# A decoder trunk in split fp32: lent weight slots in forgetting attention, and one weight split ahead of the last softmax

## The chip, the core and the metric

The kernel runs on one core of one Trainium2 chip. The metric is the device time of the program in microseconds (us), as a median of several runs. Engines are named as the profile names them: PE (TensorE matmul), PEld (its weight load), DVE (VectorE), ACT (ScalarE), POOL (GpSimd), SP (SyncE, which issues nearly all DMAs).

## The reference

Sequence 256, width 1024, two layers. Layer 0 mixes with forgetting attention (FoX, 16 heads of 64), layer 1 with multi-head latent attention (MLA, 16 heads, 128 + 64 wide). Every layer is

```python
x = post_norm(x, 0.5 * swiglu(x, ffn1_w_in[i], ffn1_w_out[i]), ln_g[i, 0], ln_b[i, 0])
mix = fox_mixer(...) if i < N_A else mla_mixer(...)
x = post_norm(x, mix, ln_g[i, 1], ln_b[i, 1])
x = post_norm(x, 0.5 * swiglu(x, ffn2_w_in[i], ffn2_w_out[i]), ln_g[i, 2], ln_b[i, 2])
gate = sigmoid(x @ ple_w_gate[i] + ple_b_gate[i])
x = post_norm(x, gate * (p[i] @ ple_w_proj[i]), ln_g[i, 3], ln_b[i, 3])
```

where post_norm is layer_norm(ALPHA * x + delta). FoX's logits are q.k / sqrt(64) plus a running sum of log sigmoid gates; both attentions are causal softmaxes. All in float32.

## The kernel before, in words

**Split arithmetic.** Every float32 operand of a matmul is written as a high part (rounded to the format fp32r) and a low part (the rest). A product is three matmuls: high x high, high x low, low x high (`mm3`). So each weight that arrives from HBM has to be split before TensorE can use it: ACT copies it rounded into the high half of a buffer (line 194, or 202 when only this half is issued), DVE subtracts this from the raw weight into the low half (line 195, or 206). One such split of a 128x1024 weight is called a split below. Activations are split in the same way (lines 499 and 500).

**Buffers.** Raw weights land in three buffers `raw`, 1 MB each, two weights to a buffer. Split weights go into slots: ten fixed ones `hl0` to `hl9`, and buffers of other use that are lent for a time (`S.lend`) and taken back (`S.reclaim`): `ota` and `otb` (later the attention's output), `qk` (later the heads' q and k) and `fs` (scratch of the FoX gates). A slot comes free when the last matmul that reads it is issued; the list of free slots is first in, first out.

**The order of the work.** The program is written out once, with a planner (class `Stream`) that decides where splits stand. After nearly every matmul group it asks (`pump`): is a slot free, has the next raw weight arrived by the planner's clock, are ACT and DVE not too far behind? If so, the next split is issued there, on ACT and on DVE. A finished pair of splits frees a raw buffer and issues the next load on SP. So the splits run ahead of TensorE as far as slots allow. In parts where ACT and DVE have other urgent work, `S.hold` turns this off, and splits stand where the code says. In MLA a list of steps (`ORDER`) says everything: `f n` splits whatever keeps the next n weights ready, `a` issues the ACT half of one split, `l` the DVE half, `sm h` is the softmax of head h (two min-reductions on DVE, line 1466, then two exponentials on ACT, line 1471), `div h 0` divides by the sums (DVE, lines 1480 and 1483), `T h` transposes the result P on TensorE and splits it into `PT`, `AV h` multiplies by V, `O h t` by one weight of the output projection, for half t of the 256 tokens.

**FoX.** It follows the first FFN. That FFN ends with the layer norm of the first 128 tokens, the transposes of these tokens into `xT` in two halves (each split on ACT and DVE), and the layer norm of the other 128. FoX then makes V in pieces: `VA(0)`, `VC(0)` (with the transposes of the other 128 tokens inside), `VB(0)`, `VC(1)`, `VB(1)`, `VA(1)`. `VC` also gives the gates' logits, which go through a chain of small steps on ACT, POOL and DVE in `fs` (lines 944 to 979). Then `gen_k` and `gen_q` make k and q of two heads at a time into `qk`, and the softmaxes follow; `AV(j)` writes the output into `ota` (j below 4) and `otb` (j from 4 on), lines 1114 and 1117.

Before, `qk` and `fs` are taken back in the first FFN (at its chunk 8), `ota` and `otb` where FoX begins.

Of the kernel before, what the change touches and what calls it, by code (L numbers as in the profile page):

```python
# [11 lines left out]
F32R = mybir.dt.float32r  # L12
# [61 lines left out]
)  # L74
# [16 lines left out]
class Recorder:  # L91
# [10 lines left out]
    lend = reclaim = check = load = busy = pair = split = split_pieces = ahead = later = split_now = fill = pump  # L102
# [295 lines left out]
class Trunk:  # L398
# [459 lines left out]
    def fox(self, li):  # L858
        nc, S, a = self.nc, self.S, self.a
        v = {}  # L860
        S.reclaim("ota", "otb")

        def VA(t):

            ps = self.bank("h" if t == 0 else "y")
            self.moving(ps, t, ("fv",), 512)
            o = v[t, 0] = self.tl([128, 2, 512], F32R, "g4", 5)
            self.parts(o[:, 0, :], o[:, 1, :], ps)

        def VB(t, what=None):  # L870

            ps = self.bank("h" if t == 0 else "y")
            for k in range(8):
                if k == 1 and what:
                    what()
                if k % 4 == 0:
                    w = self.use(("fvb", k // 4))
                c = 256 * (k % 4)
                self.mm3(
                    ps[:, 0:256], lambda i: self.xT[:, t, i, k, :], lambda i: w[:, i, c : c + 256], k == 0, k == 7)  # L880
            if (t, 1) not in v:
                v[t, 1] = self.tl([128, 2, 512], F32R, "g4", 5)
            o = v[t, 1]
            self.parts(o[:, 0, 0:256], o[:, 1, 0:256], ps[:, 0:256])

        def VC(t, at={}):

            ps = self.bank("y")
            for k in range(8):
                if k in at:  # L890
                    at[k]()
                if k % 3 == 0:
                    w = self.use(("fvc", k // 3))
                c = 272 * (k % 3)
                self.mm3(
                    ps[:, 0:272], lambda i: self.xT[:, t, i, k, :], lambda i: w[:, i, c : c + 272], k == 0, k == 7)
            if (t, 1) not in v:
                v[t, 1] = self.tl([128, 2, 512], F32R, "g4", 5)
            o = v[t, 1]
            nc.scalar.activation(ftok[:, t, 112:128], ps[:, 256:272], AF.Copy)  # L900
            self.parts(o[:, 0, 256:512], o[:, 1, 256:512], ps[:, 0:256])
# [15 lines left out]
        fs = self.own([128, 2048], F32, "fs")  # L917
# [15 lines left out]
        f, e, u, r, ab = (fs[fr, 256 * i : 256 * i + 256] for i in range(5))  # L933
# [60 lines left out]
        VC(0, {4: lambda: self.XT(1, (0,)), 7: lambda: self.XT(1, (1,))})  # L994
        VB(0)
        VC(1)
        VB(1, gates)
        VA(1)

        st, PT = {}, {}  # L1000
        qk = self.own([128, 2, 2, 512], F32R, "qk")
        OT = [self.own([128, 4, 2, 256], F32R, tag) for tag in ("ota", "otb")]

        def gen(j, key, c0, hold):
            ps = self.bank("h")
# [4 lines left out]
        def gen_k(j):  # L1010
            gen(j, "fk", 256, j >= 2)

        def gen_q(j):
            gen(j, "fq", 0, j >= 2)

        def QK(j, ring):
            sb = [self.bank(ring) for _ in range(2)]
            half = [slice(0, 64), slice(64, 128)]
            o = qk[:, j % 2]
            for s in range(2):  # L1020
                h = 2 * j + s
                self.mm(
                    sb[s][:, 0:384], sel[half[s], h : h + 1].to_broadcast([64, 128]), negc[half[s], :],
                    True, False,
                )
            for n, (i, jj) in enumerate(((0, 0), (0, 1), (1, 0))):
                for q0, c0, c1 in ((0, 0, 128), (128, 128, 384)):
                    for s in range(2):
                        self.mm(
                            sb[s][:, c0:c1], o[half[s], i, q0 : q0 + 128],  # L1030
                            o[half[s], jj, 256 : 256 + c1 - c0], False, n == 2 and q0 > 0,
                        )
            st[j] = sb
# [20 lines left out]
        def exps(j):  # L1054
            sb, tt = st[j]
            su = self.tl([128, 4], F32, "su", 2)
            pair = self.tl([128, 768], F32, "P", 2)
            P = [pair[:, 384 * s : 384 * s + 384] for s in range(2)]
            for s in range(2):
                for q, (c0, c1) in enumerate(seg):  # L1060
                    i = 2 * s + q
                    nc.scalar.activation(
                        P[s][:, c0:c1], sb[s][:, c0:c1], AF.Exp, bias=tt[:, i : i + 1], scale=-1.0,
                        accum_out=su[:, i : i + 1],
                    )
            self.S.busy(act=1800)
            st[j] = P, su
# [28 lines left out]
        def AV(j, what=None):  # L1096
            o = PT.pop(j)
            ps = self.bank("h" if j != 5 else "tr")
            n, c = j // 4, 128 * (j % 4)
            strided = ps.rearrange("p (s c) -> p s c", s=2)[:, :, 128:256]  # L1100
            for m, (i, jj) in enumerate(((0, 0), (0, 1), (1, 0))):
                self.mm(ps, v[0, n][:, i, c : c + 128], o[:, jj, 0:512], m == 0, False)
            for m, (i, jj) in enumerate(((0, 0), (0, 1), (1, 0))):
                self.mm(
                    strided, v[1, n][:, i, c : c + 128],
                    o[:, jj, 512:768].rearrange("p (s c) -> p s c", s=2), False, m == 2,
                )
            if what:
                what()
            ot = OT[j // 4][:, j % 4]  # L1110
            self.S.busy(act=700, dve=600)
            for s in range(2):
                r = slice(64 * s, 64 * s + 64)
                nc.scalar.activation(ot[r, 0, :], ps[r, 256 * s : 256 * s + 256], AF.Copy)
            for s in range(2):
                r = slice(64 * s, 64 * s + 64)
                nc.vector.tensor_tensor(
                    ot[r, 1, :], ps[r, 256 * s : 256 * s + 256], ot[r, 0, :].bitcast(F32), op=ALU.subtract
                )
# [5 lines left out]
        def O(k, t):  # L1125
# [3 lines left out]
            for n in range(2):  # L1129
                if t == 1 and k == 7:  # L1130
                    self.XT(0, (n,))
                self.mm3(
                    y[t][n], lambda i: OT[k // 4][:, k % 4, i, 128 * t : 128 * t + 128],
                    lambda i: w[:, i, 512 * n : 512 * n + 512], k == 0, k == 7,
# [8 lines left out]
        for a in range(0, 6, 2):  # L1143
            if a == 2:
                self.load_gb(li, 1)
            QK(a, "y")
            QK(a + 1, "y")
            least(a)
            if a:
                AV(a - 1)  # L1150
            exps(a)
            S.ahead()
            least(a + 1)
            gen_k(a + 2)
            exps(a + 1)
            divide(a)
            S.later()
            gen_q(a + 2)
            divide(a + 1)
            S.split_now()  # L1160
            S.split_now()
            gen_k(a + 3)
            T(a)
            S.split_now()
            gen_q(a + 3)
            AV(a)
            T(a + 1)
# [100 lines left out]
    def mla(self, li):  # L1268
# [231 lines left out]

        OT = []

        def ot_of(h):
            if h >= 14:
                return self.kvt[:, 512 * (h - 14) : 512 * (h - 13)].rearrange("p (i c) -> p i c", i=2)
            return OT[h >= 10][:, (h + 2 * (h >= 10)) % 4]

        def AV(h):
            if h in (0, 10):
                OT.append(self.own([128, 4, 2, 256], F32R, "ota" if h else "otb"))  # L1510
            o = PT.pop(h)
# [45 lines left out]
    def run(self):  # L1557
        S = self.S
        keep = lambda *t: (lambda: S.reclaim(*t))
        ple = lambda li: {  # L1560
            4: [keep("ota")],
            6: [lambda: self.ple_load(li)],
        }
        self.ffn(0, "ffn1", 0, at={3: [self.load_x], 8: [keep("qk", "fs")]}, cold=True)
        self.fox(0)
        self.ffn(0, "ffn2", 2, ple=True, at=ple(0))
        self.load_gb(0, 3)
        self.kv_setup()
        self.ple(0, False)
        S.reclaim("fs")  # L1570
        self.ffn(1, "ffn1", 0, kv=True, at={10: [keep("ota")]})
        self.mla(1)
        self.ffn(1, "ffn2", 2, ple=True, at=ple(1))
        self.load_gb(1, 3)
        self.ple(1, True)
# [94 lines left out]
```

## Time and profile before

| what | value |
|---|---|
| median of three runs | 1072.36 us (1070.35 to 1072.91) |
| the profiled execution | 1070.54 us |
| its span, first to last instruction | 1068.8 us |
| mean granted TensorE clock | 0.997 |
| PE busy | 1057.0 us (99%), 7236 matmuls |
| DVE busy | 717.7 us (67%) |
| ACT busy | 541.8 us (51%) |
| POOL busy | 64.6 us (6%) |
| HBM read | 197.40 MB, 186 GB/s over the span |

How to read it: "busy" is the union of an engine's instructions. Matmuls are pipelined, so one that waits a little still overlaps the one before it; a lost moment on PE shows in the distance from the start of one group to the start of the next. In a timeline row stand the start, the duration, engine, line, operation, what is written from what, its shape and how many equal instructions follow each other; in brackets the engine's idle time before it and what ended that. The FoX stage lies at about 188 to 303 us, MLA at about 711 to 848 us.

### The profile page before, as it was taken

How to read it: one execution, taken by the hardware profiler on the slowest of the kernel's cores; microseconds unless marked ns; L12 is line 12 of the kernel's file. 1: busy time of each engine (PE TensorE's matmuls, PEld its weight loads, DVE VectorE, ACT ScalarE, POOL GpSimd, SP SyncE). 2: the span in 40 equal slices, each digit the busy share in tenths (PEclk: the TensorE clock that was granted, in tenths of full speed). 3: DMA queues.
4: the chain of work that ended last, by engine and by line, in shares of the span. 5: the costliest groups of instructions: out<-in, count | busy, mean ns of one | idle time of the engine just before them, and what ended most of it. 6: DMA issues, size and time to landing. Idle time of an engine off the chain costs nothing.

```text
span 1068.8 us, 17497 instructions
## 1 busy us (share of the span) xinstructions
PE 1057.0 (99%) x7236; PEld 969.8 (91%) x7236; DVE 717.7 (67%) x1029; ACT 541.8 (51%) x805; POOL 64.6 (6%) x94
## 2 busy tenths in 40 slices
PE   9999999999999999999999999999999999999996
PEld 8989998899889999998899999989999789898986
DVE  6675545878797545548966454578887886454566
ACT  5654433667645534444555453436675466354431
POOL 0000000233200000000320000000000000000000
PEclk9999999999999999999999999999999999999998
DMA  8886642543347755354477555423434568555502
GB/s 298 327 286 226 242 161 83 200 163 147 119 163 289 265 192 189 141 201 148 175 277 266 182 188 182 153 71 109 148 135 153 197 239 310 178 209 179 190 5 79
DMA packets 33091, 199.58 MB, mean 187 GB/s; under 512 B 3698, under 2 KB 5490, under 8 KB 12148
## 3 DMA queue, kind: packets, MB, share of 16 engines
q1 hardware_dynamic: 33012, 198.47, 51.5%
q8 instruction: 57, 0.93, 0.3%
q14 instruction: 22, 0.18, 0.0%
HBM read 197.40 MB, written 1.05 MB: 186 GB/s over the span
## 4 chain that ended last, share of the span: by engine, by line
PE 96%; DVE 1%; issue 1%; ACT 1%; POOL 0%; DMA 0%; SPq 0%; DVEq 0%; POOLq 0%; ACTq 0%
PE y L490 36%; PE h L490 35%; PE tr L490 23%; PE tr L494 2%; DMA raw<-in_w_dram 0%; PE h L494 0%; PE tr L1086 0%; ACT hl L194 0%; DVE x L575 0%; POOL fs L957 0%; POOL fs L950 0%; SPq L360 0%; SPq L476 0%; DVE hl L195 0%; ACT P L1471 0%
## 5 line engine op out<-in xcount | busy, mean ns | idle before, releaser
L195 DVE TENSOR_TENSOR hl<-raw,hl 128x1024 fp32r<-128x1024 f32 (+3 forms) x263 | 309.2, 1195 | 143.1 <-ACT hl L194 142.4
L194 ACT ACTIVATE hl<-raw 128x1024 fp32r<-128x1024 f32 (+3 forms) x263 | 266.1, 1033 | 173.8 <-PE y L490 94.8
L490 PE MATMUL h<-xT,hl 128*128 128x256 f32 x1560 | 184.8, 278 | 1.5 <-ACT hl L232 1.2
L490 PEld LDWEIGHTS h<-xT,hl 128*128 128x128 f32 x1560 | 181.0, 188 | 2.8 <-ACT hl L232 1.5
L490 PE MATMUL y<-hl,g 128*128 128x512 f32 x780 | 182.3, 390 | 0.0
L490 PE MATMUL tr<-xT,hl 128*128 128x256 f32 x1512 | 176.6, 277 | 0.0
L490 PEld LDWEIGHTS tr<-xT,hl 128*128 128x128 f32 x1512 | 174.2, 188 | 0.5
L490 PEld LDWEIGHTS y<-hl,g 128*128 128x128 f32 x780 | 145.4, 188 | 29.5
L490 PE MATMUL h<-hl,xT 128*128 128x512 f32 (+2 forms) x300 | 67.6, 377 | 0.0
L490 PE MATMUL y<-hl,xT 128*128 128x512 f32 (+3 forms) x348 | 64.1, 334 | 0.0
L490 PEld LDWEIGHTS h<-hl,xT 128*128 128x128 f32 x300 | 53.6, 188 | 10.2
L490 PEld LDWEIGHTS y<-hl,xT 128*128 128x128 f32 x348 | 53.5, 188 | 6.3 <-ACT xT L499 0.4
L567 POOL TENSOR_TENSOR rs<-ve,mhalf 128x1 f32<-128x1 f32 x16 | 15.1, 942 | 625.9 <-DVE ve L566 625.9
L500 DVE TENSOR_TENSOR g<-P,g 128x512 fp32r<-128x512 f32 x38 | 26.3, 692 | 26.5 <-ACT g L499 26.5
L490 PE MATMUL y<-hl,otb 128*128 128x512 f32 x168 | 42.9, 396 | 0.0
L499 ACT ACTIVATE xT<-tr 128x512 fp32r<-128x512 f32 x28 | 16.2, 597 | 51.0 <-PE tr L494 50.9
L499 ACT ACTIVATE g<-P 128x512 fp32r<-128x512 f32 x38 | 24.0, 632 | 32.8 <-DVE P L684 32.8
L195 DVE TENSOR_TENSOR otb<-raw,otb 128x1024 fp32r<-128x1024 f32 (+1 forms) x21 | 25.3, 1204 | 16.7 <-ACT otb L194 16.7
L195 DVE TENSOR_TENSOR qk<-raw,qk 128x1024 fp32r<-128x1024 f32 (+2 forms) x22 | 26.6, 1211 | 14.5 <-ACT qk L194 14.4
L490 PEld LDWEIGHTS y<-hl,otb 128*128 128x128 f32 x168 | 30.2, 188 | 5.6
L683 ACT ACTIVATE P<-tr 128x512 f32<-128x512 f32 x20 | 12.0, 599 | 44.5 <-PE tr L490 44.5
L684 DVE TENSOR_TENSOR P<-P,tr 128x512 f32<-128x512 f32 x20 | 13.8, 688 | 30.0 <-PE tr L490 15.2
(262 smaller groups left out, 1432.0 us busy)
## 6 DMA issues: line engine op xcount, KB each, us to landing
raw<-in_ffn_in_dram SPq DMA_DIRECT2D x85, 1024.0 KB, 5.0
raw<-in_ffn_out_dram SPq DMA_DIRECT2D x44, 1024.0 KB, 5.0
raw<-in_pg_dram SPq DMA_DIRECT2D x8, 1024.0 KB, 4.8
raw<-in_mo_dram SPq DMA_DIRECT2D x8, 1024.0 KB, 4.8
raw<-in_kq_dram SPq DMA_DIRECT2D x8, 640.0 KB, 4.0
gb<-in_ln_g_dram SPq DMA_DIRECT2D x8, 512.0 KB, 7.0
gb<-in_ln_b_dram SPq DMA_DIRECT2D x8, 512.0 KB, 7.7
raw<-in_fk_dram SPq DMA_DIRECT2D x4, 1024.0 KB, 5.2
```

Of the source, the lines that this page charges most:

```text
L194: nc.scalar.activation(hi, src, AF.Copy)
L195: nc.vector.tensor_tensor(lo, src, hi.bitcast(F32), op=ALU.subtract)
L490: self.nc.tensor.matmul(out, lhsT, rhs, start=start, stop=stop)
L494: self.nc.tensor.transpose(out, in_, self.ident)
L499: self.nc.scalar.activation(hi, src, AF.Copy)
L500: self.nc.vector.tensor_tensor(lo, src, hi.bitcast(F32), op=ALU.subtract)
L567: nc.gpsimd.tensor_tensor(rs, ve, self.mhalf, op=ALU.pow)
L683: nc.scalar.activation(gt, ps[0], AF.Silu)
L684: nc.vector.tensor_tensor(gt, gt, ps[1], op=ALU.mult)
```

## The change

Three edits to where buffers are lent, and one to the list of steps.

1. `qk` stays lent until FoX begins and is taken back there; `ota` is taken back after `VC(1)`, `otb` at the second pair of heads (where the next layer norm's weights are loaded), and the tiles in `ota` and `otb` are made where `AV` first writes them. `fs` is taken back at chunk 10 of the first FFN.
2. In MLA, the split of the last output weight is issued as `a` ahead of `O 13 0` and `sm 15`, and its DVE half as `l` behind `sm 15`; before it stood as a whole (`f 2`) behind `sm 15`.

```diff
-    "f 1", "div 14 0", "l", "O 12 0", "AV 13", "O 6 1", "f 2", "QK 15", "T 14", "lend", "O 13 0", "sm 15",
-    "f 2", "div 15 0", "l", "AV 14", "O 7 1", "f 3", "O 8 1", "gb", "T 15", "f 4", "O 9 1", "AV 15", "O 14 0",
+    "f 1", "div 14 0", "l", "O 12 0", "AV 13", "O 6 1", "f 2", "QK 15", "T 14", "lend", "a", "O 13 0", "sm 15",
+    "l", "div 15 0", "AV 14", "O 7 1", "f 3", "O 8 1", "gb", "T 15", "f 4", "O 9 1", "AV 15", "O 14 0",
...
     def fox(self, li):
-        S.reclaim("ota", "otb")
+        S.reclaim("qk")
...
         VC(1)
+        S.reclaim("ota")
         VB(1, gates)
...
-        OT = [self.own([128, 4, 2, 256], F32R, tag) for tag in ("ota", "otb")]
+        OT = []
...
+            if j % 4 == 0:
+                OT.append(self.own([128, 4, 2, 256], F32R, "otb" if j else "ota"))
             ot = OT[j // 4][:, j % 4]
...
                 self.load_gb(li, 1)
+                S.reclaim("otb")
...
-        self.ffn(0, "ffn1", 0, at={3: [self.load_x], 8: [keep("qk", "fs")]}, cold=True)
+        self.ffn(0, "ffn1", 0, at={3: [self.load_x], 10: [keep("fs")]}, cold=True)
```

No instruction is added or taken out on PE, ACT, DVE, POOL or SP, apart from what follows from names; PE, POOL and SP keep their order, and PE reads some weights from other slots. What moves are splits on ACT and DVE.

**The end of MLA, on ACT.** P, su and nm are the probabilities, the sums and the minima of a softmax, PT the transposed and split probabilities, `fs` here the output of head 14. Before, from the split of the weight ahead of it to the head's output:

```order
L194 ACTIVATE hl9_8382<-raw_8156 128x1024
L499 ACTIVATE PT_8400<-tr_8396 128x384
L1471 ACTIVATE P_8411,su_8410<-tr_8385,nm_8409 128x128
L1471 ACTIVATE P_8411,su_8410<-tr_8385,nm_8409 128x256
L194 ACTIVATE hl6_8416<-raw_8156 128x1024
L499 ACTIVATE fs_6382<-h_8424 128x256
```

and in the changed kernel (line 1475 is line 1471 of before):

```order
L194 ACTIVATE hl6_8382<-raw_8156 128x1024
L499 ACTIVATE PT_8400<-tr_8396 128x384
L202 ACTIVATE hl2_8403<-raw_8156 128x1024
L1475 ACTIVATE P_8413,su_8412<-tr_8385,nm_8411 128x128
L1475 ACTIVATE P_8413,su_8412<-tr_8385,nm_8411 128x256
L499 ACTIVATE fs_6382<-h_8424 128x256
```

The copy of the last output weight has moved from behind the two exponentials to ahead of them. On DVE the order is as it was: the two reductions of the softmax, the subtraction of this weight, the reciprocal, the divisions.

**The start of FoX, on ACT.** `xT` is the transposed input, `g4` a piece of V, raw widths of 544 and 1024 are weights. Before, from the last splits of V's weights to the second pair of `xT` halves:

```order
L194 ACTIVATE hl4_1859<-raw_1611 128x544
L194 ACTIVATE hl5_1867<-raw_1723 128x1024
L194 ACTIVATE hl6_1876<-raw_1723 128x1024
L499 ACTIVATE xT_72<-tr_1881 128x512
L499 ACTIVATE xT_72<-tr_1891 128x512
L194 ACTIVATE hl7_1901<-raw_1788 128x1024
L499 ACTIVATE g4_1956<-h_1931 128x512
L499 ACTIVATE xT_72<-tr_1972 128x512
L194 ACTIVATE hl8_1985<-raw_1788 128x1024
L499 ACTIVATE xT_72<-tr_1993 128x512
```

and in the changed kernel:

```order
L194 ACTIVATE hl3_1790<-raw_1611 128x544
L194 ACTIVATE hl4_1864<-raw_1699 128x1024
L194 ACTIVATE hl5_1873<-raw_1699 128x1024
L499 ACTIVATE xT_72<-tr_1881 128x512
L194 ACTIVATE hl6_1891<-raw_1755 128x1024
L499 ACTIVATE xT_72<-tr_1894 128x512
L499 ACTIVATE g4_1956<-h_1931 128x512
L194 ACTIVATE hl7_1972<-raw_1755 128x1024
L499 ACTIVATE xT_72<-tr_1977 128x512
L194 ACTIVATE hl8_1993<-raw_1793 128x1024
L499 ACTIVATE xT_72<-tr_1996 128x512
```

Here the splits of the first two weights of k (hl6 and hl7, before hl7 and hl8) have each moved ahead of an `xT` half, and the first weight of q (hl8) stands ahead of the last half. The 544-wide split stands ahead of the layer norm's work on DVE in the changed kernel; before it stood behind it:

```order
L575 SCALAR_TENSOR_TENSOR x0_66<-x0_66,mv_1828,gb_648 128x512
L575 SCALAR_TENSOR_TENSOR x0_66<-x0_66,rs_1830,gb_648 128x512
L195 TENSOR_TENSOR hl4_1859<-raw_1611,hl4_1859 128x544
L195 TENSOR_TENSOR hl5_1867<-raw_1723,hl5_1867 128x1024
L195 TENSOR_TENSOR hl6_1876<-raw_1723,hl6_1876 128x1024
L500 TENSOR_TENSOR xT_72<-tr_1881,xT_72 128x512
L500 TENSOR_TENSOR xT_72<-tr_1891,xT_72 128x512
L195 TENSOR_TENSOR hl7_1901<-raw_1788,hl7_1901 128x1024
L556 SCALAR_TENSOR_TENSOR x1_67<-x1_67,y_110 128x512
```

(DVE before, from the end of the first layer norm to the start of the second), and in the changed kernel:

```order
L575 SCALAR_TENSOR_TENSOR x0_66<-x0_66,mv_1833,gb_648 128x512
L575 SCALAR_TENSOR_TENSOR x0_66<-x0_66,rs_1835,gb_648 128x512
L195 TENSOR_TENSOR hl4_1864<-raw_1699,hl4_1864 128x1024
L195 TENSOR_TENSOR hl5_1873<-raw_1699,hl5_1873 128x1024
L500 TENSOR_TENSOR xT_72<-tr_1881,xT_72 128x512
L195 TENSOR_TENSOR hl6_1891<-raw_1755,hl6_1891 128x1024
L500 TENSOR_TENSOR xT_72<-tr_1894,xT_72 128x512
L556 SCALAR_TENSOR_TENSOR x1_67<-x1_67,y_110 128x512
```

One subtraction fewer stands between the two layer norms, and one of 1024 now stands between the two halves of `xT`.

From there to about 373 us every split stands where the split of the weight before it stood: the kernel is one weight further ahead. The order of all other work on these engines is the same.

## The prediction

> **What bounds the kernel now.** I read the page first, then the waits of PE alone, then timelines of the places where splits move. On the page one engine is busy all the time, and the chain of work that ended last runs through it.
>
> ```profile
> span 1068.8 us, 17497 instructions
> PE 1057.0 (99%) x7236; PEld 969.8 (91%) x7236; DVE 717.7 (67%) x1029; ACT 541.8 (51%) x805; POOL 64.6 (6%) x94
> PE 96%; DVE 1%; issue 1%; ACT 1%; POOL 0%; DMA 0%; SPq 0%; DVEq 0%; POOLq 0%; ACTq 0%
> ```
>
> The changed kernel has the same matmuls, so only moments in which PE waits can be won. The view of PE's waits has four groups. Three belong to the program's first 9 us, which the change does not touch (one is shown), and one does not:
>
> ```profile
> PE y L466 <- POOL mhalf L450: 1.2, 1, 1.2
> ...
> PE tr L494 <- DVE P L1483: 0.8, 1, 0.8
> ```
>
> That is a single wait near the end of MLA: the transposes of the last head (T 15) wait for the division of its softmax. Shorter waits show only as a longer distance between the starts of groups, so I looked for these in timelines. In no group after the first 9 us does PE wait for a weight's split. Being one weight further ahead in FoX can therefore win nothing by itself; it can only shift what ACT and DVE do at the few places where PE is close behind them.
>
> **The start of FoX.** The timeline from the end of the first layer norm:
>
> ```profile
> 184.66 2.99 DVE L195 TENSOR_TENSOR hl<-raw,hl 128x544 fp32r<-128x544 f32 x3
> ...
> 186.19 0.60 ACT L499 ACTIVATE xT<-tr 128x512 fp32r<-128x512 f32 x1 [2.10 <-PE tr L494]
> ...
> 187.57 1.28 DVE L500 TENSOR_TENSOR xT<-tr,xT 128x512 fp32r<-128x512 f32 x2
> ...
> 187.82 1.68 PE L490 MATMUL h<-ota,xT 128*128 128x512 f32 x6
> 188.90 1.22 DVE L195 TENSOR_TENSOR hl<-raw,hl 128x1024 fp32r<-128x1024 f32 x1
> 189.33 1.54 PE L490 MATMUL h<-otb,xT 128*128 128x512 f32 x6
> 190.04 0.68 DVE L556 SCALAR_TENSOR_TENSOR x<-x,y 128x512 f32<-128x512 f32 x1
> 190.71 2.91 PE L490 MATMUL h<-hl,xT 128*128 128x512 f32 x12
> ```
>
> The first six matmuls of VA(0) take 189.33 - 187.82 = 1.51, the next six 190.71 - 189.33 = 1.38, or 0.23 each. So 0.13 is lost: the third matmul needs the low half of xT, which DVE starts at 187.57, behind three subtractions. One of them, 544 wide (about 0.6 of the 2.99), is done before the layer norm now, so this low half starts near 186.95. Gain **0.10**.
>
> Against that, a weight of k is now split between the two halves of xT: copied on ACT from 186.79 (186.19 + 0.60) for about 1.05, and subtracted on DVE for 1.22. The second half's high part starts at 187.85 and its low part ends near 187.85 + 1.22 + 0.68 = 189.75; before it ended at 188.85. PE's first reader is the third unit of VA(0), at 190.71, and wants the low part two matmuls later, at 191.17. That leaves 1.4, so the edit costs nothing; were the cover gone, it would cost at most the 1.22. The second pair of halves is used by VC(1), 10 us later, with one subtraction more ahead of it: the same price, more cover. The second layer norm starts 0.3 before 190.04; what follows it may win a tenth, which I do not count (from 0 to 0.2).
>
> From there on each split stands at an old place, one weight ahead. ACT's and DVE's queues hold as much work as before at each of them, and each load is issued sooner, since raw buffers come free sooner. Price zero, covered by PE's distance to its weights. Making the output tiles late, and `otb` holding a weight until then, puts no wait on AV, which writes it two pairs of heads later. For `fs` at chunk 10, the same weight is its last in both kernels.
>
> **The last softmax.** The timeline of MLA's end:
>
> ```profile
> 827.95 0.49 ACT L499 ACTIVATE PT<-tr 128x384 fp32r<-128x384 f32 x1 [0.91 <-PE tr L494]
> ...
> 829.08 0.80 PE L490 MATMUL h<-PT,g 128*128 128x256 f32 x6
> ...
> 829.67 0.14 DVE L1466 DVE_READ_ACCUMULATOR2_ANT nm<- 128x1 f32 x1
> 829.72 2.95 PE L490 MATMUL y<-hl,otb 128*128 128x512 f32 x12
> 829.85 0.37 ACT L1471 ACTIVATE P<-tr,nm 128x128 f32<-128x128 f32 x1 [1.41 <-DVE nm L1466]
> ...
> 830.56 0.20 ACT L1471 ACTIVATION_READ_ACCUMULATOR P<-tr,nm 128x1 f32 x1
> 830.66 1.05 ACT L194 ACTIVATE hl<-raw 128x1024 fp32r<-128x1024 f32 x1
> ...
> 831.74 1.22 DVE L195 TENSOR_TENSOR hl<-raw,hl 128x1024 fp32r<-128x1024 f32 x1 [1.93 <-ACT hl L194]
> ...
> 832.88 0.16 DVE L1480 RECIPROCAL su<-su 128x2 f32<-128x2 f32 x1
> 833.08 0.55 DVE L1483 TENSOR_SCALAR P<-P,su 128x128 f32<-128x128 f32 x2
> ...
> 833.51 0.61 PE L494 MATMUL tr<-ident,P 128*128 128x128 f32 x3 [0.84 <-DVE P L1483]
> 833.54 0.42 DVE L500 TENSOR_TENSOR fs<-h,fs 128x256 fp32r<-128x256 f32 x1
> 833.87 1.22 DVE L195 TENSOR_TENSOR hl<-raw,hl 128x1024 fp32r<-128x1024 f32 x1
> 833.88 1.64 PE L490 MATMUL y<-hl,otb 128*128 128x512 f32 x6
> 834.22 0.49 ACT L499 ACTIVATE PT<-tr 128x384 fp32r<-128x384 f32 x1 [1.28 <-PE tr L494]
> ...
> 835.01 0.55 DVE L500 TENSOR_TENSOR PT<-tr,PT 128x384 fp32r<-128x384 f32 x1
> 835.35 1.05 PE L490 MATMUL h<-PT,g 128*128 128x256 f32 x6
> ```
>
> The sums of the softmax are there at 830.76 (830.56 + 0.20), yet DVE's reciprocal starts at 832.88. Ahead of it in DVE's queue stands the subtraction of a weight, and that waits for its copy, which ACT makes only behind the exponentials. PE's twelve 512-wide matmuls from 829.72 take 12 x 0.23 = 2.76, so T 15 could have started at 832.48; it started at 833.51. PE loses **1.03**.
>
> Now the copy stands ahead of the exponentials. ACT is done with PT at 828.44 and idle for 1.41 until 829.85. The copy takes 1.05 and ends at 829.49, 0.36 before the exponentials can start, so they lose nothing. Its raw weight is the other half of a buffer that was split from a head earlier. DVE's last reduction ends at 829.81; the subtraction runs from there to 831.05, beside the exponentials, and the reciprocal starts at 831.05, 1.83 earlier. The transposes could start at 833.51 - 1.83 = 831.68, and PE gets to them at 832.48. So the whole 1.03 goes, with 0.8 to spare. On SP the load that this split frees, and the next layer norm's two loads behind it, issue up to 1.9 earlier in the same order; POOL has nothing here.
>
> What is late next is head 15's AV. Its six matmuls took 1.05, those of head 14 0.80: 0.25 is lost, since the second matmul needs the low half of PT, which ended at 835.56. In the new order T 15 and PT's copy come 1.03 earlier; the copy ends at 833.68. On DVE the divisions end at 831.8, then follow 0.42 and a subtraction of 1.22, so it is free at about 833.45, and the low half ends near 834.25. AV 15 starts at 832.85 + 1.38 = 834.23 and its second matmul about 0.1 later. I take **0.20** of the 0.25.
>
> **The sum.** 0.10 + 1.03 + 0.20 = 1.33 us, all of it PE's own waiting. The profiled execution took 1070.54 (its span, and 1.7 around it), and becomes 1069.2. The median of the runs stands 1.82 above that execution: 1072.36 - 1.33 = **1071.0**, 0.12% less. The three runs lie 0.24% apart (1070.35 to 1072.91), so 0.3% (3.2 us) is about what a measurement can tell from no change.
>
> **Rivals.** *A race on the gates' chain.* FoX's gates share DVE with the first k and q:
>
> ```profile
> 212.20 11.68 PE L490 MATMUL h<-xT,hl 128*128 128x256 f32 x96
> ...
> 213.78 0.74 POOL L956 TENSOR_TENSOR fs<-fs 32x256 f32<-32x256 f32 x1 [2.94 <-DVE fs L955]
> ...
> 214.55 1.23 DVE L195 TENSOR_TENSOR hl<-raw,hl 128x1024 fp32r<-128x1024 f32 x1 [0.86 <-ACT hl L194]
> 214.59 1.79 POOL L957 TENSOR_TENSOR fs<-fs 32x256 f32<-32x256 f32 x1
> ...
> 217.66 0.42 DVE L500 TENSOR_TENSOR qk<-h,qk 128x256 fp32r<-128x256 f32 x1
> ```
>
> ```profile
> 328.67 8.43 PE L490 MATMUL tr<-xT,hl 128*128 128x256 f32 x72
> ```
>
> [...] The chain ends in the qk subtraction at 217.66, for which PE waits: 72 such matmuls take 8.43, so 96 would take 11.2 and took 11.68. [...] ACT and DVE keep their order there and move with PE, so I give a turn either way 0.15.
>
> *A load that comes late: slower.* The first weight of q's second pair is now copied at the place below, right ahead of the gates' first step on ACT:
>
> ```profile
> 198.87 0.35 SPq L368 DMA_DIRECT2D raw<-in_fq_dram  x1
> ...
> 204.17 1.06 ACT L194 ACTIVATE hl<-raw 128x1024 fp32r<-128x1024 f32 x1
> ```
>
> ```profile
> DMA to landing us min/median/max: 4.8/4.9/6.5
> ```
>
> Its issue moves from 198.87 to about 198.0, because the subtraction that frees the buffer stands one `xT` half earlier. So it has 6.2 to land; beyond that ACT holds the gates, and PE pays one for one. The longest of q's four loads (6.5) would cost 0.3. The kernel is slower than before once a landing takes 6.2 + 1.33 = 7.5; at twice the median, 9.8, it costs 3.6 (1074.6). No load of q took that long: 0.05.
>
> *The copy does not fit, and the change does not do what it says.* If the copy starts more than 0.8 after 828.44, each further moment is taken from the 1.03, and at 1.83 only FoX's 0.10 is left (1072.3). Nothing in the rows delays it: 0.10.
>
> **How the numbers follow.** The forecast has 0.58, the race 0.15, the copy 0.10, the late load 0.05. A further 0.12 is for the forecast's mechanism with a median at the low end of the runs, 1070.35 - 1.33 = 1069.0. The range starts a little above that, at 1069.2, and ends at 1072.8, which takes in the copy's case and the highest run with nothing won (1072.91) nearly. Faster by over 0.3% is below 1069.14, so 0.12; slower by over 0.3% is above 1075.6, beyond the late load's time and for things unseen, 0.06; within, 0.82.
>
> **What would show it.** In the changed profile PE no longer waits for the divisions; the subtraction ahead of head 15's reciprocal runs beside the exponentials; AV 15 takes near 0.85; VA(0)'s first six matmuls take 1.38; PE's busy time stays near 1057 and the span is about 1067.4. It is wrong if T 15 still waits, if PE waits for an xT half in VA(0), or if ACT waits for a DMA between 197 and 212 us.

## The result, and the profile after

The changed kernel takes 1069.37 us (median of 16 runs, 1068.27 to 1071.70), the kernel before 1071.20 us on the same chip (16 runs, 1070.29 to 1072.91). The ratio is 0.9986, with a 95% interval of 0.9979 to 0.9992: faster by 0.14%. That is within the 0.3% that the prediction took for what a measurement can tell from no change, but the interval excludes 1. The profiled execution took 1069.07 us.

The page of the changed kernel, its span and busy times, and then the view of PE's waits (line, what it waited for, us in total, times, longest):

```profile
span 1067.3 us, 17503 instructions
PE 1056.7 (99%) x7236; PEld 970.6 (91%) x7236; DVE 718.1 (67%) x1029; ACT 542.6 (51%) x805; POOL 68.1 (6%) x94
```

```profile
PE y L466 <- POOL mhalf L450: 1.2, 1, 1.2
PE h L490 <- DVE hl L234: 0.5, 1, 0.5
PE h L490 <- ACT hl L232: 0.3, 1, 0.3
PE h L490 <- DVE qk L500: 0.3, 1, 0.3
```

PE is as busy as before (1056.7 against 1057.0) and the span is 1.5 shorter, so what went is waiting. The wait for the divisions (0.8) is gone. The first three rows belong to the first 9 us. The fourth is the stall on the gates' chain that the prediction had found as a longer distance. The lines of the changed code are 3 or 4 higher than before: the divisions of L1483 are now L1487, the reciprocal is L1484.

The timeline of the changed kernel at the start of FoX (start, duration, engine, line, operation; in brackets the idle time before and what ended it):

```profile
187.13 0.68 DVE L500 TENSOR_TENSOR xT<-tr,xT 128x512 fp32r<-128x512 f32 x1
...
188.02 1.54 PE L490 MATMUL h<-ota,xT 128*128 128x512 f32 x6
...
189.39 1.54 PE L490 MATMUL h<-otb,xT 128*128 128x512 f32 x6
189.71 0.68 DVE L556 SCALAR_TENSOR_TENSOR x<-x,y 128x512 f32<-128x512 f32 x1
```

DVE starts the first low half of xT at 187.13 instead of 187.57. The first six matmuls take 189.39 - 188.02 = 1.37 instead of 1.51. The second layer norm starts at 189.71 instead of 190.04. Its transposes, before and then in the changed kernel:

```profile
195.16 0.63 PE L494 MATMUL tr<-ident,x 128*128 128x128 f32 x4
```

```profile
195.03 0.60 PE L494 MATMUL tr<-ident,x 128*128 128x128 f32 x4
```

The end of latent attention in the changed kernel, in the same view:

```profile
828.24 1.05 ACT L202 ACTIVATE hl<-raw 128x1024 fp32r<-128x1024 f32 x1
...
829.58 1.22 DVE L206 TENSOR_TENSOR hl<-raw,hl 128x1024 fp32r<-128x1024 f32 x1
829.63 2.95 PE L490 MATMUL y<-hl,otb 128*128 128x512 f32 x12
829.76 0.37 ACT L1475 ACTIVATE P<-tr,nm 128x128 f32<-128x128 f32 x1 [0.47 <-DVE nm L1470]
...
830.72 0.16 DVE L1484 RECIPROCAL su<-su 128x2 f32<-128x2 f32 x1
...
831.93 1.23 DVE L195 TENSOR_TENSOR hl<-raw,hl 128x1024 fp32r<-128x1024 f32 x1
...
832.42 0.49 PE L494 MATMUL tr<-ident,P 128*128 128x128 f32 x3
832.66 1.64 PE L490 MATMUL y<-hl,otb 128*128 128x512 f32 x6
...
833.53 0.56 DVE L500 TENSOR_TENSOR PT<-tr,PT 128x384 fp32r<-128x384 f32 x1 [0.38 <-ACT PT L499]
...
834.14 0.80 PE L490 MATMUL h<-PT,g 128*128 128x256 f32 x6
...
834.78 2.95 PE L490 MATMUL y<-hl,fs 128*128 128x512 f32 x12
```

The copy (L202) runs in time in which ACT was idle before, and ends 0.47 before the exponentials (L1475). The subtraction runs beside them, the reciprocal starts at 830.72 instead of 832.88, and T 15 follows the twelve matmuls with no wait. AV 15 takes 0.80 as AV 14 does.

To tell these places from the rest, I take the start of the same matmul in two traces and subtract what the start of the program differed by, measured just ahead of VA(0). The traces differ there by up to 3 us for reasons that have nothing to do with the change: up to 0.7 arises in the first 9 us, and 1.4 to 1.5 in each of two stretches in which PE is slower (last section). Behind VA(0) they repeat to about a tenth. In us, minus is earlier than the kernel before:

| profiled execution | before VA(0) | VA(0) to the end of the gates' stall | VA(0) to AV 14 | T 15 | AV 15 | sum without the first column | ratio of the times |
|---|---|---|---|---|---|---|---|
| changed | +0.20 | -0.28 | -0.29 | -1.12 | -0.25 | -1.67 | 0.9986 (0.9979 to 0.9992) |
| changed_again | -0.14 | -0.29 | -0.33 | -1.12 | -0.25 | -1.71 | 0.9985 (0.9972 to 0.9998) |
| end_only | +0.04 | 0.00 | +0.01 | -1.12 | -0.25 | -1.36 | 0.9986 (0.9976 to 0.9996) |
| fox_only | +1.54 | -0.29 | -0.18 | +0.01 | 0.00 | -0.15 | 0.9991 (0.9981 to 1.0002) |
| division_first | -0.45 | 0.00 | -0.08 | -1.12 | +0.47 | -0.71 | 0.9994 (0.9983 to 1.0005) |
| two_splits_first | +3.04 | 0.00 | -0.04 | +1.14 | -0.26 | +0.84 | one run |
| quiet_gates | +2.61 | -0.77 | +0.35 | -1.12 | -0.25 | -1.03 | 0.9989 (0.9978 to 0.9999) |
| one_split_later | +0.16 | -0.77 | -0.89 | -1.11 | -0.25 | -2.25 | 0.9986 (0.9977 to 0.9995) |
| gates_on_dve | -0.72 | -0.15 | -0.19 | -1.12 | -0.25 | -1.57 | one run |
| qk_lent_alone | +0.06 | -0.77 | -0.89 | +0.01 | -0.01 | -0.91 | one run |
| qk_and_end | +0.51 | -0.77 | -0.89 | -1.12 | -0.25 | -2.26 | 0.9975 (0.9964 to 0.9986) |

The first three columns of differences are taken at one matmul each: the first of VA(0), the one that ends the gates' stall, the first of AV 14; the second and third count from the first. The column T 15 is what is added from AV 14 to the first matmul behind the transposes of T 15, AV 15 from there to the first behind AV 15. Each is rounded for itself, so sums can be off by 0.01 or 0.02.

The times are much coarser than the traces: an interval of the table is 0.1% or about 1 us to either side. They cannot rank the kernels that differ by some tenths. one_split_later and qk_and_end gain the same in their traces (2.25 and 2.26), and their ratios are 0.9986 and 0.9975. What each place is worth is therefore read from the traces. Each trace is a single execution, but an edit gives the same value in all traces that hold it: T 15 has 1.11 or 1.12 in eight of them.

### The profile page after: what moved, and what is told of

Read it like the earlier page. It is cut to its first block, busy times and chain, and to the rows that moved or that the text cites. A ratio compares the mean times of both kernels' runs of the same rounds, so it can differ in the third digit from the quotient of the medians.

```text
span 1067.3 us, 17503 instructions
## 1 busy us (share of the span) xinstructions
PE 1056.7 (99%) x7236; PEld 970.6 (91%) x7236; DVE 718.1 (67%) x1029; ACT 542.6 (51%) x805; POOL 68.1 (6%) x94
## 3 DMA queue, kind: packets, MB, share of 16 engines
HBM read 197.40 MB, written 1.05 MB: 186 GB/s over the span
## 4 chain that ended last, share of the span: by engine, by line
PE 97%; issue 1%; POOL 0%; DVE 0%; ACT 0%; DMA 0%; SPq 0%; DVEq 0%; ACTq 0%; POOLq 0%
PE y L490 36%; PE h L490 35%; PE tr L490 23%; PE tr L494 2%; DMA raw<-in_w_dram 0%; PE h L494 0%; PE tr L1087 0%; DVE x L575 0%; POOL fs L957 0%; POOL fs L950 0%; ACT hl L194 0%; SPq L360 0%; SPq L476 0%; POOL fs L956 0%; ACT hl L232 0%
## 5 line engine op out<-in xcount | busy, mean ns | idle before, releaser
L195 DVE TENSOR_TENSOR hl<-raw,hl 128x1024 fp32r<-128x1024 f32 (+2 forms) x260 | 305.7, 1194 | 146.7 <-ACT hl L194 146.1
L194 ACT ACTIVATE hl<-raw 128x1024 fp32r<-128x1024 f32 (+2 forms) x260 | 262.9, 1031 | 183.4 <-PE y L490 97.5
L490 PEld LDWEIGHTS h<-xT,hl 128*128 128x128 f32 x1584 | 184.3, 189 | 2.5 <-ACT xT L499 0.9
L490 PE MATMUL y<-hl,g 128*128 128x512 f32 x792 | 185.6, 390 | 0.0
L490 PE MATMUL tr<-xT,hl 128*128 128x256 f32 x1464 | 170.8, 277 | 0.0
L490 PEld LDWEIGHTS tr<-xT,hl 128*128 128x128 f32 x1464 | 168.6, 188 | 0.5
L490 PE MATMUL y<-hl,xT 128*128 128x512 f32 (+3 forms) x330 | 59.7, 331 | 0.0
L490 PEld LDWEIGHTS y<-hl,xT 128*128 128x128 f32 x330 | 50.1, 188 | 5.6 <-ACT xT L499 0.4
L194 ACT ACTIVATE otb<-raw 128x1024 fp32r<-128x1024 f32 (+1 forms) x22 | 22.9, 1039 | 19.4 <-PE y L490 10.8
L194 ACT ACTIVATE qk<-raw 128x1024 fp32r<-128x1024 f32 (+2 forms) x23 | 24.0, 1045 | 16.3 <-PE tr L490 6.6
```

Of the source, the lines that this page charges most:

```text
L194: nc.scalar.activation(hi, src, AF.Copy)
L195: nc.vector.tensor_tensor(lo, src, hi.bitcast(F32), op=ALU.subtract)
L490: self.nc.tensor.matmul(out, lhsT, rhs, start=start, stop=stop)
```

## Experiments

**Each half alone.** The new order of steps at the end of latent attention, put into the kernel before:

```diff
-    ... "T 14", "lend", "O 13 0", "sm 15",
-    "f 2", "div 15 0", "l", "AV 14", ...
+    ... "T 14", "lend", "a", "O 13 0", "sm 15",
+    "l", "div 15 0", "AV 14", ...
```

> The kernel before with the new order of steps at the end of latent attention alone; the start of forgetting attention (FoX) is the old one. Theory (the gain is PE's own waiting): T 15 no longer waits and AV 15 takes 0.80 as AV 14 does, so 1.03 + 0.25 = 1.28 us go: span near 1067.5 against 1068.8, ratio near 0.9988. The stall on the gates' chain stays 0.41, since nothing ahead of it moves. Rival (being a weight ahead from FoX on carries part of the gain): less than 0.9 us, T 15 or AV 15 still late by some tenths.

Measured: span 1067.5, and in the table 1.12 + 0.25 = 1.37 at the end of latent attention and nothing elsewhere. The theory holds, to a tenth. The stall at the gates is also told wrongly in the expectation: in this trace PE stops there for 0.59 (start to start, 217.59 to 218.18), with the old FoX. The 0.41 that I had read from the kernel before is one execution's value. In that execution the 48 matmuls ahead of the stall stand 118 ns apart, here 113: PE had lost the other 0.2 there, and so came later to the same stall (the last section has more of such stretches).

The other half is the same diff taken back in the changed kernel:

> The changed kernel with the old order of steps at the end of latent attention. Theory: VA(0)'s first six matmuls 1.38, the second x transposes 0.2 earlier, a tenth of it given back at the gates' chain, whose stall grows to 0.6; T 15 waits as before (0.8 on the view of waits) and AV 15 takes 1.05: 0.2 to 0.3 us in all, span near 1068.5, ratio 0.9997, which the times alone cannot tell from 1. Rival (being a weight ahead pays at many places): 0.8 us or more, ratio 0.9993 or below, and a shorter wait at T 15.

Measured: 0.29 at the gates, the wait at T 15 as before (0.8 on the view of waits), AV 15 as before. Nothing is gained at any later place, so being a weight ahead pays at the start of FoX only. The profiled execution's span, 1070.1, is longer because of slower stretches of PE (last section). Behind the gates it also gives back 0.11 (-0.29 to -0.18, where the changed kernel has -0.28 to -0.29), by my reading in a short stretch of the same kind at 220 to 225 us, so that this trace is only 0.15 ahead at its end. The ratio, 0.9991 (0.9981 to 1.0002), decides nothing: it holds both theories. Without this loss the halves add: 0.29 + 1.37 = 1.66, and the changed kernel has 1.67.

**Which queue held T 15.** Here only DVE's order is changed: the division goes ahead of the split, whose copy stays behind the exponentials.

```diff
-    "f 2", "div 15 0", "l", "AV 14", ...
+    "div 15 0", "f 2", "l", "AV 14", ...
```

> The kernel before, with the split that stands ahead of head 15's division put behind it: on DVE the reciprocal and the two divisions come first, the copy on ACT stays behind the exponentials. Theory (DVE's queue decides, and the early copy is what lets the subtraction run beside the exponentials): T 15 starts on time, 1.03 gained, but the subtraction now runs from the copy's end (831.7) to 832.95, and with the 0.42 and the 1.22 that follow, the low half of PT ends near 835.15, 0.8 after AV 15's second matmul wants it: AV 15 takes 1.6, so only 0.4 to 0.6 us are gained, span near 1068.3. Rival (only the place against the division counts): 1.28 us, span near 1067.5, AV 15 0.8.

The timeline of this kernel:

```profile
830.28 0.17 DVE L1480 RECIPROCAL su<-su 128x2 f32<-128x2 f32 x1 [0.98 <-ACT P L1471]
...
831.23 1.23 DVE L195 TENSOR_TENSOR hl<-raw,hl 128x1024 fp32r<-128x1024 f32 x1 [0.20 <-ACT hl L194]
...
831.98 0.49 PE L494 MATMUL tr<-ident,P 128*128 128x128 f32 x3
...
832.70 1.22 DVE L195 TENSOR_TENSOR hl<-raw,hl 128x1024 fp32r<-128x1024 f32 x1
...
833.83 0.55 DVE L500 TENSOR_TENSOR PT<-tr,PT 128x384 fp32r<-128x384 f32 x1
...
834.44 0.79 PE L490 MATMUL h<-PT,g 128*128 128x256 f32 x5 [0.46 <-DVE PT L500]
```

T 15 is on time, so it was the subtraction ahead of the reciprocal that held it. But the subtraction now stands with the next one in front of PT's low half, which ends at 834.38, and AV 15's second matmul waits for it. 0.47 is lost there against the kernel before; I had expected 0.55 (1.6 against 1.05), because I laid DVE's rows end to end, while each starts about 0.09 before the one ahead of it ends (PT's low half at 833.83, the subtraction's end at 832.70 + 1.22 = 833.92). In all 0.71 is gained, above the 0.4 to 0.6 that I had expected, and well below the rival's 1.28; the ratio, 0.9994 (0.9983 to 1.0005), cannot tell it from nothing. The early copy is thus worth 0.65 us (1.36 - 0.71) beside the mere place of the division: it is what gives the subtraction an empty place on DVE.

**The same cause, doubled.** The kernel before, with the next weight split at the same place too:

```diff
-    "f 2", "div 15 0", "l", "AV 14", ...
+    "f 3", "div 15 0", "l", "AV 14", ...
```

> The kernel before, with two weights split ahead of head 15's division instead of one, the second being the one that stood right behind it. Theory (each subtraction ahead of the reciprocal, with its copy behind the exponentials, is paid by T 15 one for one): the reciprocal comes 1.1 to 1.2 later and T 15 with it; AV 15's low half no longer has that subtraction ahead, so its 0.25 comes back: 0.9 to 1.2 us slower at the end of latent attention. Rival (T 15's wait has another cause, PT's bank or the scores): T 15 as before.

PE's wait in this kernel, and DVE's queue from its timeline:

```profile
PE tr L494 <- DVE P L1483: 2.0, 1, 2.0
```

```profile
834.74 2.36 DVE L195 TENSOR_TENSOR hl<-raw,hl 128x1024 fp32r<-128x1024 f32 x2 [1.93 <-ACT hl L194]
...
837.02 0.16 DVE L1480 RECIPROCAL su<-su 128x2 f32<-128x2 f32 x1
```

Both subtractions stand between the exponentials and the reciprocal, and the wait grows from 0.8 to 2.0; T 15 costs 1.14 more, where the first subtraction had cost 1.12. Each subtraction there is paid by PE one for one. AV 15's 0.25 comes back (-0.26), since no subtraction is left in front of PT's low half. With division_first, where T 15's loss goes and AV 15's grows, this shows for both losses at the end of latent attention that a subtraction ahead in DVE's queue makes them.

**What holds PE at the gates.** The timeline of the changed kernel:

```profile
211.84 1.75 DVE L955 RECIPROCAL fs<-fs 32x256 f32<-32x256 f32 x1
...
214.46 1.23 DVE L195 TENSOR_TENSOR otb<-raw,otb 128x1024 fp32r<-128x1024 f32 x1 [0.86 <-ACT otb L194]
214.51 1.79 POOL L957 TENSOR_TENSOR fs<-fs 32x256 f32<-32x256 f32 x1
...
215.60 0.68 DVE L500 TENSOR_TENSOR g<-y,g 128x512 fp32r<-128x512 f32 x1
...
216.33 0.42 DVE L962 SCALAR_TENSOR_TENSOR fs<-fs 32x256 f32<-32x256 f32 x1
...
217.58 0.42 DVE L500 TENSOR_TENSOR qk<-h,qk 128x256 fp32r<-128x256 f32 x1
```

Two things end together in front of L962: POOL's L957, which takes 1.79 beside the subtraction (214.51 + 1.79 = 216.30), and DVE's own row (215.60 + 0.68 = 216.28). Two kernels part them. The first keeps the split and takes the work from POOL:

```diff
-                nc.gpsimd.tensor_tensor(e, e, r, op=ALU.mult)
-                nc.gpsimd.tensor_tensor(u, e, ab, op=ALU.subtract)
+                nc.vector.tensor_tensor(e, e, r, op=ALU.mult)
+                nc.vector.tensor_tensor(u, e, ab, op=ALU.subtract)
```

> The changed kernel, with the two 32x256 operations L956 and L957 on DVE instead of POOL; the weight's subtraction stays behind them. Theory (DVE's own queue sets the stall): from the reciprocal's start to the qk subtraction it was 5.74; now reciprocal 1.75, 0.42, 0.42, subtraction 1.23, g 0.68, scan steps 0.42 and 0.69 make 5.6, and the stall stays at 0.5 to 0.6. Rival (POOL's blocked 1.79 sets it): the step that waited for POOL comes 1.05 earlier, and the stall goes as it did without the subtraction.

```profile
210.93 1.75 DVE L955 RECIPROCAL fs<-fs 32x256 f32<-32x256 f32 x1
...
212.71 0.42 DVE L956 TENSOR_TENSOR fs<-fs 32x256 f32<-32x256 f32 x1
...
213.69 1.23 DVE L195 TENSOR_TENSOR otb<-raw,otb 128x1024 fp32r<-128x1024 f32 x1
...
216.79 0.42 DVE L500 TENSOR_TENSOR qk<-h,qk 128x256 fp32r<-128x256 f32 x1
```

From the reciprocal's start to the qk subtraction it is 5.86 now (216.79 - 210.93), against 5.74. The two operations run while DVE would wait for the weight's copy: its subtraction starts 2.76 behind the reciprocal's start, against 2.62. The rest of the row is as long as before, so the 1.05 that L957 takes longer on POOL beside the subtraction (1.79, against 0.74 without it in quiet_gates below) wins nothing: DVE is not free earlier either.

The second takes the split away from there. It holds weight splits back from the last quarter of VA(1) to gen_k(1):

```diff
+        def quiet():
+            S.hold = True
...
-            self.moving(ps, t, ("fv",), 512)
+            self.moving(ps, t, ("fv",), 512, 18 if t else None, quiet)
...
         gen_k(0)
+        quiet()
         gen_q(0)
```

> The changed kernel, with no weight split between the last quarter of VA(1) and gen_k(1): the subtraction of 1.23 us that starts at 214.46 beside L957, and two behind it, come later. Theory: the stall of 0.60 us ahead of gen_k(1) is DVE's queue (reciprocal 1.75, wait for the copy 0.86, subtraction 1.23, g 0.68, two scan steps, then qk); without the subtraction qk's low half comes a microsecond earlier and PE does not wait: 0.5 us less, span near 1066.8. [...] Rival (the splits that are put off are needed soon): PE waits for a weight of the second pair, and what is won is lost again, span 1067.3 or more.

Measured: the stall is gone (0.77 ahead behind the gates instead of 0.28, and 0.90 some 2 us later). L957 takes 0.74, against 1.79 beside the subtraction in the changed kernel. But two weights less are in hand from there on, and FFN2 pays for it, as the view of PE's waits and the timeline of this kernel show:

```profile
PE h L490 <- ACT hl L194: 0.9, 1, 0.9
```

```profile
311.70 2.00 ACT L194 ACTIVATE hl<-raw 128x1024 fp32r<-128x1024 f32 x2
...
312.80 1.20 PE L490 MATMUL h<-hl,xT 128*128 128x512 f32 x4 [0.92 <-ACT hl L194]
```

ACT's copies stand behind a table load (1.28, from 310.12) and a Silu (at 311.42) there, and the weight is one that PE wants now. So both theories were right, each at its place, but for where the rival's wait stands: in FFN2, not at the second pair. In all this trace gains 1.03, less than the changed kernel's 1.67. The same without the second quiet(), with one weight less in hand instead of two:

```diff
         gen_k(0)
-        quiet()
         gen_q(0)
```

> The changed kernel, with no weight split between the last quarter of VA(1) and the end of gen_k(0) only: each split from there on stands where the next one stood, one weight less ahead until FFN2. Theory: the stall ahead of gen_k(1) goes (0.5 to 0.6 us), and with one weight in hand more than in the run with the longer quiet stretch, PE does not wait for a weight at the start of FFN2: the whole 0.5 stays, span near 1066.8 where the clock is that of the runs before. Rival (any weight less in hand is paid for): PE waits at 310 us for a weight, 0.9 as in the longer stretch or a part of it, and the time is that of the changed kernel or worse.

Measured: no wait on the view but those of the first 9 us; 0.89 stays up to AV 14, 2.25 in all. One weight in hand less costs nothing, two cost 1.2. The times do not show the 0.6 that the traces have over the changed kernel: the ratio is 0.9986 (0.9977 to 0.9995), as that of the changed kernel.

**Which lent buffer gives and which takes.** The row at 214.46 writes `otb`: the split in front of the chain is one that the lending of `otb` makes room for. So I lent `qk` alone, with the old end (the edit of `fs` stays):

```diff
-        S.reclaim("ota", "otb")
+        S.reclaim("qk", "ota", "otb")
...
-        ... at={3: [self.load_x], 8: [keep("qk", "fs")]}, cold=True)
+        ... at={3: [self.load_x], 10: [keep("fs")]}, cold=True)
```

> Of the changes to FoX only the first: qk stays a weight's slot until FoX begins, ota and otb are taken back there as before, and the end of latent attention is the old one. Theory (the start's gain comes from qk alone): VA(0) gains 0.14, the x transposes 0.2, and at the gates' chain 0.1 is given back, as with all three: 0.29 ahead at 219 us, less or no more ahead later, and T 15 waits as before. Rival (ota and otb carry a part): less than 0.2.

```profile
211.71 1.75 DVE L955 RECIPROCAL fs<-fs 32x256 f32<-32x256 f32 x1
...
213.86 0.69 DVE L500 TENSOR_TENSOR g<-y,g 128x512 fp32r<-128x512 f32 x1 [0.40 <-ACT g L499]
214.35 0.74 POOL L957 TENSOR_TENSOR fs<-fs 32x256 f32<-32x256 f32 x1
...
215.12 0.42 DVE L962 SCALAR_TENSOR_TENSOR fs<-fs 32x256 f32<-32x256 f32 x1 [0.57 <-POOL fs L957]
...
216.37 0.42 DVE L500 TENSOR_TENSOR qk<-h,qk 128x256 fp32r<-128x256 f32 x1
```

Neither theory had this: the start gains the same, and then the gates gain another 0.6. With no slot free, no weight is split between the reciprocal and g, L957 takes 0.74, and the chain takes 4.66 (216.37 - 211.71) instead of 5.74. It is one execution, but the next kernel repeats it. So `qk` brings 0.9 us, and the two output buffers take 0.6 of it back. With `ota` and `otb` lent and `qk` not, the order of the instructions is that of the kernel before on every engine and in the queue of loads, so that kernel was not run.

**Both gains together.** `qk` lent alone, with the new end:

> The kernel before with qk lent until FoX and the new order of steps at the end of latent attention; ota and otb are taken back at FoX's start as before. Theory (the gains add, and the lending of otb is what cost 0.6 at the gates): 0.9 at FoX's start and 1.36 at the end, 2.25 us in all against the kernel before and 0.6 less than the changed kernel: span near 1066.6, ratio 0.9979. Rival (what FoX's start wins is lost again where the weights are one less ahead): PE waits for a weight between 220 and 330 us, and the ratio is that of the changed kernel, 0.9986.

Beside it, the changed kernel once more:

> The changed kernel once more, beside the one above on the same chip: span near 1067.3, stall ahead of gen_k(1) 0.6, T 15 on time, ratio 0.9986; both theories agree here.

Measured: 1069.09 us (11 runs) at a ratio of 0.9975 (0.9964 to 0.9986) against 0.9985 (0.9972 to 0.9998) of the changed kernel. The view of waits of the former has only the rows of the first 9 us. That it is faster than the kernel before is shown by the times; that it is 0.6 us faster than the changed kernel is what the traces show (2.26 against 1.67 and 1.71); the times do not show it, since the two intervals overlap.

## Why the prediction was right

The change came out as forecast, 0.14% faster against 0.12%, and so did the mechanism: what went is PE's waiting, at the places named, 1.67 us in the traces against 1.33. The time itself was forecast less well: 1069.37 lies 1.6 below the 1071.0, more than the whole gain, and only 0.17 above the range's lower end. The last step below says where that comes from. That the time stayed inside the range was in part luck. By the steps:

- *The last softmax, T 15: 1.03.* 1.12. The missing 0.1 is in the transposes themselves: from the start of T 15 to the next group it took 833.88 - 833.51 = 0.37 before and takes 832.66 - 832.42 = 0.24 now. Before, the three transposes start 0.17 apart, now 0.11. The second waits for its division, which ends at 833.63; why the third stands as far behind the second, the rows do not show.
- *AV 15: 0.20 of 0.25.* All of the 0.25. I had DVE free at 833.45 and PT's low half done at 834.25. DVE is free at 833.16 (831.93 + 1.23), then waits 0.38 for ACT's half of PT, and the low half ends at 834.09 (833.53 + 0.56), before AV 15 starts. The main reason is that I laid rows end to end: the subtraction starts at 829.58, not at 829.81, and the reciprocal at 830.72, not at 831.05. division_first shows the other side of this estimate.
- *The start of FoX: 0.10, and a tenth that I did not count.* 0.14, and 0.2 at the second layer norm's transposes, of which some hundredths are given back by 204 us. From the start of VA(0) to these it is 195.16 - 187.82 = 7.34 before and 195.03 - 188.02 = 7.01 now: 0.33, of which VA(0) has 0.14. That the second layer norm would start 0.3 earlier was read and left out; it belonged in the sum, which would have been 1.5 instead of 1.33.
- *Each split stands at an old place: price zero.* Right against the kernel before, and the step where I saw least. One of the old places, the one in front of the gates' chain, cost 0.6 us already. Lending `qk` would have emptied it; lending `otb` filled it again. A price against before is not a price against what the change could have been.
- *The race at the gates: 0.15 for a turn either way.* The order of the two starts did not turn there, and that this order decides how long POOL takes is shown by no run. What the runs show is a longer time beside the subtraction: L957 takes 1.79 in the kernel before and in the changed kernel, where DVE's row starts first (214.55 against 214.59, and 214.46 against 214.51), and 0.74 in the four executions without a subtraction of a weight there (quiet_gates and one_split_later, at line 960 there, qk_lent_alone, qk_and_end). At L931, where POOL's row starts first, both a long and a short time occur (last section). Nor would a shorter L957 alone have won anything: in the changed kernel DVE's own row ended 0.02 before L957, and gates_on_dve, which takes the work from POOL, has the stall still (0.3 on the view of PE's waits, as in the changed kernel). I had watched POOL's chain alone, one of two that end together.
- *The late load.* The load issues at 197.94, and its copy at 204.06 waits for no DMA.
- *The copy does not fit.* It starts at 828.24, 0.2 before the 828.44 that I had worked out, and fits with 0.47 to spare.
- *The median: 1.82 above the profiled execution.* With 16 runs the kernel before has 1071.20, 0.66 above. From there the forecast would have been 1069.9, against 1069.37. Two of the three runs that I had were among the three slowest of the 16.

## What to carry to other kernels

Where PE is busy 99% of the time, look for the places where another engine's row stands in front of one that PE waits for; here a subtraction of 1.22 us that waits for its copy in front of a reciprocal cost PE 1.12, and a second one 1.14 more. Room for one more weight is not good by itself: ask at which place of each queue the split that it allows will stand. Where two chains end together, price both before calling either the bound: here they ended within 0.02 us of each other, and taking POOL's away alone won nothing. And where runs of one kernel lie 0.3% apart, a gain of 0.1% is found by comparing the starts of the same matmul in two traces, place by place.

## What the runs showed that was not expected

The profiled executions of fox_only and quiet_gates had long stretches ahead of VA(0) in which PE alone is 4% slower, while the granted clock in the same row reads 1.00. From 25 to 60 us (busy time and count of PE, PEld, DVE, ACT and POOL, then the clock, the DMA share and GB/s), first the changed kernel, then fox_only, then quiet_gates:

```profile
25.00:60.00 35.00, 35.00 (x311) 35.00 (x310) 23.52 (x23) 18.89 (x22) 0.00 (x0) 1.00 0.85 318
```

```profile
25.00:60.00 35.00, 35.00 (x298) 34.89 (x298) 25.37 (x25) 20.14 (x24) 0.00 (x0) 1.00 0.83 315
```

```profile
25.00:60.00 35.00, 35.00 (x299) 35.00 (x299) 24.43 (x24) 19.08 (x23) 0.00 (x0) 1.00 0.85 315
```

The matmuls of 256 stand 113 ns apart in the first (35.00 / 311) and 117 in the others (35.00 / 298 and 35.00 / 299). DVE's instructions take 1.02, 1.01 and 1.02 us on average in the three rows, ACT's 0.86, 0.84 and 0.83, so these two are not slower. The stretch of 35 us costs 1.5 us in fox_only (13 matmuls fewer) and 1.4 in quiet_gates (12 fewer), nearly as much as the whole change. The programs are the same there (fox_only differs from the changed kernel only behind 820 us, quiet_gates only behind 200). Shorter ones stand in the FoX stage: from 212 us on in the kernel before, where the matmuls ahead of the stall stand 118 ns apart against 113 in the changed kernel, and at 211 in gates_on_dve, where the 48 matmuls ahead of the stall take 5.82 against 5.63 in end_only. The long ones are where the column before VA(0) gets most of fox_only's 1.54 and half of quiet_gates' 2.61 from. That the rest of that, the 3.04 of two_splits_first and the spread of the times come from such stretches too is likely, but not shown. What they are stays open.

A tiny operation on POOL takes 1.10 longer in some executions than in others, about as much as the 1.05 of L957, and which it is can turn from one execution to the next. The changed kernel's timeline, and then that of fox_only, whose instructions are the same here:

```profile
196.37 0.23 POOL L930 TENSOR_TENSOR fs<-fs,ident 128x16 f32<-128x16 f32 x1
...
196.67 1.32 POOL L931 TENSOR_TENSOR sel<-fs,ident 128x16 fp32r<-128x16 f32 x1
196.69 1.22 DVE L195 TENSOR_TENSOR hl<-raw,hl 128x1024 fp32r<-128x1024 f32 x1
```

```profile
198.00 0.22 POOL L931 TENSOR_TENSOR sel<-fs,ident 128x16 fp32r<-128x16 f32 x1
198.04 1.26 DVE L195 TENSOR_TENSOR hl<-raw,hl 128x1024 fp32r<-128x1024 f32 x1
```

L931 takes 0.22 or 1.32. POOL's row starts first in both, by 0.02 in the one and by 0.04 in the other; in the second DVE's row is 0.04 longer. In changed_again L931 takes 1.31 and starts 0.03 before DVE's row of 1.21; in quiet_gates (line 934 there) it takes 0.22 and starts 0.03 before DVE's row of 1.27. So POOL starts first in all four, it takes long in two and short in two, and 0.03 stands on both sides: which of the two it will be is not to be read from starts that lie so close. A turn like the one that the prediction feared at L957 happens here, with POOL's start recorded first each time. It costs nothing: the changed kernel and fox_only are equally far ahead behind the gates (0.28 and 0.29).
